# Two mixture-of-experts stages: three more weight units loaded before the router, gathers placed among the expert pairs, and the order of products fixed

## The chip, the cores and the metric

The kernel runs on one core of one Trainium2 chip. The metric is device time in microseconds (us) of one execution, the median of several runs. One execution has also been taken by the hardware profiler; times below that name a place in the run are counted from the first instruction of that execution.

## What is computed

The input is 256 tokens of 1024 numbers (two tiles of 128 tokens), all in float32. Two blocks follow each other. The first has two layers (l = 0, 1), and each layer is

```python
x = layer_norm(ALPHA * x + attention_mixer(x))          # ln1
x = layer_norm(ALPHA * x + moe(x))                      # ln2
```

The mixer joins three kinds of attention and a product with `w_out`. The mixture of experts (moe) sends each token to 2 of 16 experts, chosen by a sigmoid router; an expert is `down(silu(x @ gate) * (x @ up))` with `gate` and `up` of 1024 x 512 and `down` of 512 x 1024. So the weights of an expert are three matrices of 2 MB, 96 MB for the 16 experts of a layer. The second block (two feed-forward layers each with its own mixer and a cross attention to a memory) uses the first block's output, and a matrix `mem_wkv_2`, of which a quarter is multiplied at the beginning and another at the end of each moe stage of the first block.

## The kernel before, in words

The kernel is written in a language in which Python code states the instructions and their data, and a scheduler chooses, for each engine, the order in which they are issued. An instruction stated later can be issued earlier, if its inputs and its buffer are there. `self.after(x)` (L461) fixes an order by hand: the instructions stated inside it come behind x on x's engine. Every engine and every queue works through its own list in order.

**Weights.** Class `Stream` (L82 to L176) holds one list of all weight loads in the order of use. A unit is one DMA of up to 1 MB on SyncE's queue (L122). Units go into one of two rings of 8 KB per partition: `stage` (NSTAGE = 6 slots) and `piece` (NPIECE = 6). For most products a unit in `stage` is split by ScalarE (L146) and VectorE (L147) into a high and a low part, which stand in a slot of `piece`. The units of the experts and of the memory matrix are "raw": they are used as they are, in float32, straight from either ring. An expert unit is half of a matrix, 1 MB; experts of even number use `stage`, those of odd number `piece` (L342, L347). `take` (L165) hands out the next unit, `release` (L172) gives its slot back, and `_load` (L116) issues, in the order of the list, all loads that have a slot. The list of a layer is made in `plan` (L312): the blocks of `w_in`, the other weights of the mixer, four units of `w_out`, two units of the memory matrix, then for each pair of experts four units of `gate`, four of `up` and (one pair later) four of `down`, then the first block of the next weights and two more memory units.

**The mixer's end.** `mixer` (L784) makes its last block of projections at L985, with the low half of its input in buffer `xl`. It turns the queries and keys of the last attention into buffer `m4` (L986 to L992), runs that attention (L994) and multiplies with `w_out` (L1008).

**The router and the gathers.** `moe` (L1173) computes the router, the place of each token in its expert's list of 64 (CAP) tokens, and a selection matrix. `gather(g)` (L1271) multiplies the normalised tokens (buffers `m5` and `m2`) with columns of that matrix and so collects the tokens of four experts into a buffer: `m0`, `m1`, `xh`, `xl` for g = 0 to 3. One gather is 32 products of 256 columns. `memory_gemm` (L1686) is the memory product of this stage's beginning; it is stated at L1292.

**The expert stage.** The loop at L1367 goes over eight pairs of experts and one turn more. A product of a pair runs two experts side by side: expert k writes rows 64k to 64k+63 of the result, so two instructions with 64 weight columns each occupy the two halves of TensorE. In float32 an instruction is shown as two steps. A turn `pr` does: `gate` of pair `pr` (L1316), the transposes of the previous pair's activations (L1332), other work of that turn, the scatter of pair `pr-2` (L1360), `up` of pair `pr` (L1316), `down` of pair `pr-1` (L1345). In turn 0 the other work is gather(1), in turn 1 gather(2), gather(3) and eight pairs of transposes of the selection matrix (L1390) into buffer `m5`. In front of turn 2 a value is loaded and tested (L1369, L1370); the code under the test, `moe_more` (L1424), handles lists of more than 64 tokens and does not run with this input. After the last turn the result is normalised (`LayerNorm.tile` for both tiles, L1404 and L1406), and the memory product of the stage's end is made (L1419).

Of the kernel before, what the change touches and what calls it, by code (L numbers as in the profile page):

```python
# [16 lines left out]
P = 128  # L17
# [6 lines left out]
NSTAGE = 6  # L24
# [57 lines left out]
class Stream:  # L82
# [3 lines left out]
    def __init__(self, nc, stage_pool, piece_pool):  # L86
        self.nc, self.pools = nc, (stage_pool, piece_pool)
# [3 lines left out]
        self.rings = ([], [])  # L91

# [8 lines left out]
    def raw(self, key, ap, a, b, ring):  # L101

        self.units.append(dict(ap=ap, a=a, b=b, left=1, tile=None, ring=ring, first=len(self.pieces)))
        self.pieces.append(dict(key=key, u=len(self.units) - 1, raw=True, n=len(self.pieces)))
# [11 lines left out]
    def _load(self, upto=None):  # L116
        while self.loaded < (upto or len(self.units)):
            u = self.units[self.loaded]
            if not self._room(u["ring"]) or u["ring"] and u["first"] > self.split:
                return  # L120
            u["tile"] = self._tile(u["ring"], u)[:, :u["a"] * u["b"]].rearrange("p (a b) -> p a b", a=u["a"])
# [57 lines left out]
class LayerNorm:  # L179
# [8 lines left out]
    def tile(self, t):  # L188
        k = self.k
        if self.full:  # L190
# [3 lines left out]
            self.copied = k.x_t(self.res[:, t, :], t, self.hi, self.lo, self.g)  # L194
            return
# [56 lines left out]
class Kern:  # L252
    def __init__(self, ctx, tc, I, out, consts_ap, coff, bands_ap, stop=None):
# [23 lines left out]
        self.ws = Stream(nc, self.sp, self.wp)  # L277
# [29 lines left out]

    def sm(self, n, name, dt=F32, bufs=None):
        return self.small.tile([P, n], dt, name=name, tag=name, bufs=bufs)


    def plan(self):  # L312
        I, ws = self.I, self.ws
        for l in range(2):
# [20 lines left out]
            mem(1024 * l)  # L335
            for k in range(9):
                if k < 8:
                    for name in ("gate", "up"):
                        for j0 in (0, 4):
                            for e in (2 * k, 2 * k + 1):  # L340
                                w = I["exp_w_" + name][l, e].rearrange("(p j) n -> p j n", j=8)
                                ws.raw(name, w[:, j0:j0 + 4], 4, 512, e % 2)  # L342
                if k > 0:
                    for c0 in (0, 2):
                        for e in (2 * k - 2, 2 * k - 1):
                            w = I["exp_w_down"][l, e].rearrange("(p c) n -> p c n", c=4)
                            ws.raw("down", w[:, c0:c0 + 2], 2, 1024, e % 2)  # L347
# [152 lines left out]
    def x_t(self, src, t, hi, lo, g=None, b=None):  # L500
# [3 lines left out]
        for q in range(2):  # L504
            p = self.mm()
            for k in range(4):
                nc.tensor.transpose(p[:, k * P:(k + 1) * P], src[:, 4 * q + k:D:8], self.c["ident"])
# [62 lines left out]
    def spread_gb(self, g, b, l):  # L570

        nc = self.nc
        row = self.slot("m1").rearrange("p (k d) -> p k d", k=2)
# [1650 lines left out]
```

## Time and profile before

| | us |
|---|---|
| median of 3 runs | 2030.56 |
| lowest and highest of them | 2025.97, 2030.61 |
| the profiled execution, its own time | 2032.96 |
| its span, first to last instruction | 2031.2 |
| router of layer 0 to its first expert product | 158 to 187.7 |
| expert stage of layer 0, first product to last scatter | 187.7 to 423.0 |
| expert stage of layer 1, first product to last scatter | 602.4 to 837.2 |

TensorE is busy in 96% of the span, VectorE in 56%, ScalarE in 43%; the granted TensorE clock is 0.98 of full speed on the mean. The DMA engines move 453 MB, 223 GB/s on the mean. The share of busy time is a mean over stages with different limits, and an engine counts as busy also where it works at half its width; so the stage that is changed has to be read by itself.

### The profile page before, as it was taken

What the parts mean: (1) busy time and instruction counts of PE and PEld (TensorE: products, weight loads), DVE (VectorE), ACT (ScalarE), POOL (GpSimd) and SP (SyncE); (2) the same over time, 40 slices, a digit from 0 to 9 for tenths busy, and PEclk for the clock granted to TensorE, in tenths of its full rate; (3) what the DMA queues carried; (4) which work ended last, traced back from release to release, by engine and by line L of the source; (5) the groups of instructions that cost most, each with busy time, mean ns of one, the idle gap of its engine ahead of it and who ended that gap; (6) DMA issues with size and microseconds to landing.
All of it is one profiled execution on the core that took longest, in us unless ns stands there. A gap on an engine that the chain in (4) does not pass through costs nothing.

```text
span 2031.2 us, 27990 instructions
## 1 busy us (share of the span) xinstructions
PE 1952.2 (96%) x11069; PEld 1472.9 (73%) x11069; DVE 1128.5 (56%) x2211; ACT 868.5 (43%) x1537; POOL 56.6 (3%) x115
## 2 busy tenths in 40 slices
PE   6999899989999999899999899999999999999999
PEld 6776433358764333389989787899989986778998
DVE  7775122157761122556569776655565567756554
ACT  5553100036632000345456565644454455556442
POOL 1110000000100000000000100000000000000000
PEclk9999999999999999999999999999999997999999
DMA  8347899974469999955555344465555553325551
GB/s 271 138 144 264 351 413 422 420 257 147 146 221 368 393 420 421 361 190 184 194 167 186 105 187 145 146 206 189 185 182 184 187 190 135 125 83 185 188 187 42
DMA packets 175980, 453.39 MB, mean 223 GB/s; under 512 B 11056, under 2 KB 106780, under 8 KB 149084
## 3 DMA queue, kind: packets, MB, share of 16 engines
q1 hardware_dynamic: 172044, 435.55, 58.2%
q0 software_dynamic: 3792, 15.91, 2.2%
q8 instruction: 91, 1.49, 0.3%
q14 instruction: 53, 0.43, 0.1%
HBM read 446.19 MB, written 5.24 MB: 222 GB/s over the span
## 4 chain that ended last, share of the span: by engine, by line
PE 58%; DMA 5%; DVE 3%; ACT 2%; issue 1%; POOL 0%; SPq 0%; DVEq 0%; ACTq 0%; POOLq 0%
PE mm L1563 7%; PE mm L1564 7%; PE mm L1565 7%; PE accb L451 4%; PE accb L450 4%; PE accb L449 4%; PE acca L451 4%; PE acca L450 4%; PE acca L449 4%; PE mm L1316 2%; DMA piece<-in_exp_w_down_dram 2%; DMA piece<-in_exp_w_gate_dram 2%; DMA piece<-in_exp_w_up_dram 1%; DVE piece L147 1%; PE mm L1808 1%; PE acca L1345 1%
## 5 line engine op out<-in xcount | busy, mean ns | idle before, releaser
L147 DVE TENSOR_TENSOR piece<-stage,piece 128x1024 fp32r<-128x1024 f32 (+3 forms) x439 | 514.7, 1181 | 253.6 <-ACT piece L146 251.7
L146 ACT ACTIVATE piece<-stage 128x1024 fp32r<-128x1024 f32 (+3 forms) x439 | 445.6, 1023 | 342.8 <-PE mm L1565 204.1
L1563 PE MATMUL mm<-m,piece 128*128 128x256 f32 x736 | 206.9, 281 | 2.3 <-DVE m L2121 2.3
L1564 PE MATMUL mm<-m,piece 128*128 128x256 f32 x736 | 206.7, 281 | 0.0
L1565 PE MATMUL mm<-m,piece 128*128 128x256 f32 x736 | 206.4, 280 | 0.0
L1563 PE MATMUL mm<-xh,piece 128*128 128x256 f32 x576 | 163.1, 283 | 0.0
L1565 PE MATMUL mm<-xh,piece 128*128 128x256 f32 x576 | 163.0, 283 | 0.0
L1564 PE MATMUL mm<-xl,piece 128*128 128x256 f32 x576 | 163.0, 283 | 0.0
L449 PE MATMUL accb<-piece,m 128*128 128x512 f32 (+1 forms) x364 | 143.8, 396 | 1.2 <-ACT m L916 1.0
L450 PE MATMUL accb<-piece,m 128*128 128x512 f32 (+1 forms) x364 | 144.8, 398 | 0.0
L451 PE MATMUL accb<-piece,m 128*128 128x512 f32 (+1 forms) x364 | 143.7, 395 | 0.5 <-DVE m L459 0.5
L1563 PEld LDWEIGHTS mm<-m,piece 128*128 128x128 f32 x736 | 139.2, 189 | 4.6 <-issue 3.0
L1564 PEld LDWEIGHTS mm<-m,piece 128*128 128x128 f32 x736 | 139.2, 189 | 1.9 <-issue 0.3
L1565 PEld LDWEIGHTS mm<-m,piece 128*128 128x128 f32 x736 | 139.4, 189 | 0.0
L449 PE MATMUL acca<-piece,m 128*128 128x512 f32 (+1 forms) x348 | 137.1, 395 | 1.8 <-ACT m L458 1.6
L450 PE MATMUL acca<-piece,m 128*128 128x512 f32 (+1 forms) x348 | 137.7, 396 | 0.0
L451 PE MATMUL acca<-piece,m 128*128 128x512 f32 (+1 forms) x348 | 137.1, 395 | 0.5 <-DVE m L459 0.5
L1316 PE MATMUL mm<-stage,m 128*64 128x512 f32 x256 | 122.2, 630 | 7.9 <-DVEq L1370 6.3
L1316 PE MATMUL mm<-piece,m 128*64 128x512 f32 x256 | 121.6, 631 | 3.3 <-issue 3.3
L1563 PEld LDWEIGHTS mm<-xh,piece 128*128 128x128 f32 x576 | 110.4, 192 | 1.3
L1564 PEld LDWEIGHTS mm<-xl,piece 128*128 128x128 f32 x576 | 110.4, 192 | 1.2
L1565 PEld LDWEIGHTS mm<-xh,piece 128*128 128x128 f32 x576 | 110.4, 192 | 0.0
(573 smaller groups left out, 3745.0 us busy)
## 6 DMA issues: line engine op xcount, KB each, us to landing
stage<-in_ffn_wi_dram SPq DMA_DIRECT2D x88, 1024.0 KB, 5.4
stage<-in_ffn_wo_dram SPq DMA_DIRECT2D x44, 1024.0 KB, 5.2
stage<-in_exp_w_gate_dram SPq DMA_DIRECT2D x32, 1024.0 KB, 7.0
stage<-in_exp_w_up_dram SPq DMA_DIRECT2D x32, 1024.0 KB, 9.5
piece<-in_exp_w_gate_dram SPq DMA_DIRECT2D x32, 1024.0 KB, 14.6
piece<-in_exp_w_up_dram SPq DMA_DIRECT2D x32, 1024.0 KB, 13.0
stage<-in_exp_w_down_dram SPq DMA_DIRECT2D x32, 1024.0 KB, 15.0
piece<-in_exp_w_down_dram SPq DMA_DIRECT2D x32, 1024.0 KB, 18.8
```

Of the source, the lines that this page charges most:

```text
L146: nc.scalar.activation(wh, src, AF.Copy)
L147: nc.vector.tensor_tensor(wl, src, wh.bitcast(F32), op=OP.subtract)
L449: nc.tensor.matmul(out, ah, bh, start=first, stop=False)
L450: nc.tensor.matmul(out, ah, bl, start=False, stop=False)
L451: return nc.tensor.matmul(out, al, bh, start=False, stop=last)
L1316: mm = nc.tensor.matmul(o[64 * k:64 * k + 64, :], x[:, j, s:s + CAP], w[k][:, jj, :], start=(j == 0), stop=(j == 7))
L1345: nc.tensor.matmul(y[nb][64 * k:64 * k + 64, :], x[:, f, 64 * k:64 * k + 64], w[k][:, cc, nb * 512:(nb + 1) * 512], start=(f == 0), stop=( ...
L1563: nc.tensor.matmul(out, wh[:, j, :], hi[:, j, :], start=(j == 0), stop=False)
L1564: nc.tensor.matmul(out, wh[:, j, :], lo[:, j, :], start=False, stop=False)
L1565: nc.tensor.matmul(out, wl[:, j, :], hi[:, j, :], start=False, stop=(j == 7))
L1808: nc.tensor.matmul(po[:, k * P:(k + 1) * P], v[:, mc, h * 256 + cc * P:h * 256 + (cc + 1) * P], pt[t][:, (2 * h + mc) * P:(2 * h + mc + 1) ...
```

## The change

It has seven parts.

1. NSTAGE is 7 instead of 6, for the whole kernel. The room comes from `dynamic_dma_scratch_size=8192` at the kernel's end.
2. Two units, the first halves of `gate` of experts 0 and 1, no longer use the rings. They go into the buffers `xl` and `m4`, once these are free of the mixer's data (`ws.free += ...` is stated behind L992). In the list the first of them stands in front of the `w_out` units, the second behind them; `_load` stops at such a unit until its buffer has been set free.
3. The other expert units alternate between the rings in a cycle of 13.
4. Inside one `gate`, `up` or `down` every product is put behind the one before it, so the two experts of a pair alternate strictly.
5. gather(2) moves from turn 1 to turn 2 and gather(3) to turn 4. The gathers alternate between `m0` and `m1`. The transposed selection matrix goes to `xl`, the scatter's input to `xh` instead of `m2`, since `m5`, `m2` are needed longer.
6. The test of L1370 moves from turn 2 to turn 4.
7. At the end of the stage the order is fixed: first half of the memory product, transposes of the normalised tile 0, second half of the memory product, transposes of tile 1, then the memory product's copies out. The table for the square root is loaded on ScalarE behind the last `silu`. The memory product's results go to other buffers, and to DRAM in two DMAs of GpSimd's queue instead of one.

```diff
-NSTAGE = 6
+NSTAGE = 7
 class Stream:
+    def raw(self, key, ap, a, b, ring=0, slot=None):
+        self.units.append(dict(ap=ap, a=a, b=b, left=1, tile=None, ring=ring, slot=slot, first=len(self.pieces)))
+        u = len(self.units) - 1
+        if not slot:
+            self.use(key, u)
+        return u
+    def use(self, key, u):
+        self.pieces.append(dict(key=key, u=u, raw=True, n=len(self.pieces)))
     def _load(self, upto=None):
         while self.loaded < (upto or len(self.units)):
             u = self.units[self.loaded]
-            if not self._room(u["ring"]) or u["ring"] and u["first"] > self.split:
+            if u.get("slot"):
+                if u["slot"] not in self.free:
+                    return
+                self.free.remove(u["slot"])
+                t = self.slot(u["slot"])
+            elif not self._room(u["ring"]) or u["ring"] and u["first"] > self.split:
                 return
+            else:
+                t = self._tile(u["ring"], u)
...
     def plan(self):
+            early = lambda e, tag: ws.raw("gate", I["exp_w_gate"][l, e].rearrange("(p j) n -> p j n", j=8)[:, 0:4], 4, 512,
+                                          slot=tag)
+            first = [early(0, "xl")]
             self.plan_rows("w_out", I["w_out"][l].rearrange("(c p) n -> p c n", p=P), 8)
+            first.append(early(1, "m4"))
...
+            def expert(key, ap, a, b):
+                nonlocal n
+                ws.raw(key, ap, a, b, n % (NSTAGE + NPIECE) % 2)
+                n += 1
...
     def mixer(...):
                 nc.vector.tensor_copy(qkfT[:66, k, :, t * P:(t + 1) * P], p[:66].rearrange("p (b n) -> p b n", b=4))
+        ws.free += ["xl", "m4"]
...
     def moe(...):
-            x = self.slot(("m0", "m1", "xh", "xl")[g]).rearrange("p (j n) -> p j n", j=8)
+            x = self.slot(("m0", "m1")[g % 2]).rearrange("p (j n) -> p j n", j=8)
...
         def gate_or_up(kind, pr):
+            prev = []
...
-                        mm = nc.tensor.matmul(o[64 * k:64 * k + 64, :], x[:, j, s:s + CAP], w[k][:, jj, :],
-                                              start=(j == 0), stop=(j == 7))
+                        with self.after(*prev):
+                            mm = nc.tensor.matmul(o[64 * k:64 * k + 64, :], x[:, j, s:s + CAP], w[k][:, jj, :],
+                                                  start=(j == 0), stop=(j == 7))
+                        prev = [mm]
...
         for pr in range(9):
-            if pr == 2:
+            if pr == 4:
                 more = nc.values_load(ovi[0:1, 0:1], min_val=0, max_val=1)
...
             if pr == 1:
-                gather(2)
-                gather(3)
-                ptr = self.slot("m5", F32R).rearrange("p (a n) -> p a n", a=8)
+                ptr.append(self.slot("xl", F32R).rearrange("p (a n) -> p a n", a=8))
...
+            if pr == 2:
+                gather(2)
+            if pr == 4:
+                gather(3)
...
                 scatter(7, y)
-                nxt.tile(0)
-                ready = nxt.copied
-                nxt.tile(1)
...
-        self.memory_gemm(l, 1, "m0", after={0: [state["scatter"]]}, out_after=ready)
+        with self.after(state["silu"]):
+            self.table(AF.Sqrt)
+        def first(at):
+            with self.after(at):
+                nxt.tile(0)
+            return nxt.moved
+        at = self.memory_gemm(l, 1, [m0[:, 512 * t:512 * t + 512] for t in range(2)], {0: [state["scatter"]]}, first, l)
+        with self.after(at):
+            nxt.tile(1)
+        self.memory_out(nxt.copied)
...
-    nc = _bacc.Bacc("TRN2", target_bir_lowering=False, num_devices=1)
+    nc = _bacc.Bacc("TRN2", target_bir_lowering=False, num_devices=1, dynamic_dma_scratch_size=8192)
```

`down` gets the same chain of `self.after(*prev)`; `moe_more` is rewritten for the new buffers.

## Rows read from the trace of the kernel before

**Rows 1.** The page: the span in 40 slices of 50.8 us, DMA's busy tenths.
```profile
DMA  8347899974469999955555344465555553325551
```

**Rows 2.** Stretches of layer 0's expert stage: busy time by engine, clock, DMA share, GB/s.
```profile
190.00:200.00 10.00, 10.00 (x53) 5.01 (x50) 0.78 (x3) 1.73 (x3) 0.00 (x0) 0.89 0.54 203
200.00:220.00 20.00, 20.00 (x114) 10.23 (x113) 4.50 (x9) 3.51 (x7) 0.00 (x0) 1.00 0.97 395
220.00:240.00 20.00, 20.00 (x112) 9.88 (x110) 3.59 (x7) 5.07 (x10) 0.00 (x0) 1.00 0.76 303
240.00:260.00 20.00, 13.68 (x54) 5.35 (x53) 4.46 (x7) 1.55 (x3) 0.00 (x0) 0.83 0.95 382
...
340.00:360.00 20.00, 19.65 (x82) 7.96 (x80) 5.49 (x8) 1.20 (x2) 0.00 (x0) 1.00 1.01 420
```

**Rows 3.** DMA issues of 187 to 424 us: count, KB each, median us to landing.
```profile
piece<-in_exp_w_down_dram SPq DMA_DIRECT2D x16, 1024.0 KB, 18.8
stage<-in_exp_w_up_dram SPq DMA_DIRECT2D x14, 1024.0 KB, 12.2
...
stage<-in_exp_w_gate_dram SPq DMA_DIRECT2D x12, 1024.0 KB, 14.0
```

**Rows 4.** SyncE's queue in order of time: start us, us, what.
```profile
60.90 34.53 SPq L122 DMA_DIRECT2D stage<-in_w_out_dram  x4
...
193.61 0.33 SPq L122 DMA_DIRECT2D stage<-in_exp_w_up_dram  x1
...
197.04 0.33 SPq L122 DMA_DIRECT2D stage<-in_exp_w_up_dram  x1
...
396.11 0.33 SPq L122 DMA_DIRECT2D piece<-in_exp_w_down_dram  x1
```

**Rows 5.** TensorE in order of time, start of layer 0's expert stage.
```profile
187.66 1.11 PE L1316 MATMUL mm<-stage,m 128*64 128x512 f32 x1
187.67 1.11 PE L1316 MATMUL mm<-piece,m 128*64 128x512 f32 x1
...
195.99 0.59 PE L1316 MATMUL mm<-stage,m 128*64 128x512 f32 x1
...
196.42 0.59 PE L1316 MATMUL mm<-stage,m 128*64 128x512 f32 x1
...
196.94 0.39 PE L1282 MATMUL mm<-gv,m 128*128 128x256 f32 x1
...
201.12 0.64 PE L1316 MATMUL mm<-stage,m 128*64 128x512 f32 x1
...
246.90 1.08 PE L1316 MATMUL mm<-stage,m 128*64 128x512 f32 x1 [6.32 <-DVEq L1370]
```

**Rows 6.** TensorE's groups of 187 to 424 us: busy us, mean ns, idle before.
```profile
L1360 PE MATMUL mm<-m,m 128*128 128x512 f32 x64 | 22.3, 442 | 1.9 <-DVE res L1362 0.6
...
L1332 PE MATMUL tp<-ident,prob 128*128 128x128 f32 x32 | 6.0, 310 | 0.1
```

**Rows 7.** TensorE in order of time, end of layer 0's expert stage.
```profile
420.28 2.81 PE L1360 MATMUL mm<-m,m 128*128 128x512 f32 x8
...
434.60 1.97 PE L507 MATMUL mm<-ident,res 128*128 128x128 f32 x8 [5.31 <-DVE res L562]
```

**Rows 8.** Stretches of layer 1's expert stage, columns as in rows 2.
```profile
640.00:660.00 20.00, 15.87 (x69) 5.03 (x69) 2.13 (x3) 1.97 (x4) 0.00 (x0) 1.00 0.78 311
660.00:680.00 20.00, 19.19 (x73) 8.14 (x74) 3.08 (x5) 0.60 (x1) 0.00 (x0) 0.83 0.93 349
```

**Rows 9.** Stretches ahead of layer 0's expert stage, columns as in rows 2.
```profile
125.00:146.00 21.00, 19.50 (x115) 15.02 (x114) 17.54 (x59) 12.50 (x36) 0.00 (x0) 1.00 0.38 144
...
173.00:193.00 20.00, 20.00 (x103) 13.25 (x103) 11.97 (x32) 4.93 (x7) 2.84 (x5) 0.83 0.41 119
```

**Rows 10.** TensorE in order of time: `w_out` products, and the last attention's end.
```profile
123.57 0.40 PE L449 MATMUL accb<-piece,m 128*128 128x512 f32 x1
...
144.58 0.50 PE L1134 MATMUL tp<-pt,m 128*64 128x128 f32 x3
```

More of the change, by code (lines that the diff above doesn't have):

```diff
@@ L91, in __init__ @@
         self.rings = ([], [])
+        self.free = []
     def unit(self, ap, a, b):
@@ L340, in plan @@
                             for e in (2 * k, 2 * k + 1):
+                                if first:
+                                    ws.use("gate", first.pop(0))
+                                    continue
                                 w = I["exp_w_" + name][l, e].rearrange("(p j) n -> p j n", j=8)
-                                ws.raw(name, w[:, j0:j0 + 4], 4, 512, e % 2)
+                                expert(name, w[:, j0:j0 + 4], 4, 512)
                 if k > 0:
@@ L346, in plan @@
                             w = I["exp_w_down"][l, e].rearrange("(p c) n -> p c n", c=4)
-                            ws.raw("down", w[:, c0:c0 + 2], 2, 1024, e % 2)
+                            expert("down", w[:, c0:c0 + 2], 2, 1024)
             if l == 0:
@@ L568, in ln_gain, with spread_gb @@
         self.nc.vector.tensor_tensor(v, v, gb[1], op=OP.add)
[L570 removed]
+    def spread_gb(self, g, b, l, tag):
         nc = self.nc
[L573 removed]
+        row = self.slot(tag).rearrange("p (k d) -> p k d", k=2)
         for k, v in enumerate((g, b)):
@@ L1291, in moe @@
             ln.gain(rows)
-        self.memory_gemm(l, 0, "xl", {7: [at_pp]})
+        self.memory_gemm(l, 0, [self.prob()[:, 0:512] for t in range(2)], {7: [at_pp]})
         p = self.tp()
@@ L1683, in memory_load, with memory_gemm @@
         self.nc.gpsimd.dma_start(self.mem_t, self.memT)
-    def memory_gemm(self, k, b, tag, after={}, out_after=()):
-        o = self.slot(tag)[:, 0:D].rearrange("p (t d) -> p t d", t=2)
-        acc = [self.acc(), self.acc()]
+    def memory_gemm(self, k, b, out, after={}, mid=None, pair=None):
+        acc = [self.acc(pair), self.acc(pair)]
         x = self.mem_t.rearrange("p (j n) -> p j n", j=8)
@@ L1691, in memory_gemm @@
             for j in range(8):
+                if j == 4 and mid:
+                    order.enter_context(self.after(mid(at)))
                 if j in after:
@@ L1696, in memory_gemm, with memory_out @@
                 for t in range(2):
-                    self.nc.tensor.matmul(acc[t], x[:, j, t * P:(t + 1) * P], w[:, j % 4, :], start=(j == 0), stop=(j == 7))
+                    at = self.nc.tensor.matmul(acc[t], x[:, j, t * P:(t + 1) * P], w[:, j % 4, :], start=(j == 0), stop=(j == 7))
                 if j % 4 == 3:
                     self.ws.release()
-        with ExitStack() as order:
-            order.enter_context(self.after(*out_after))
+        self.mem_out = (k, b, acc, out)
+        if not mid:
+            self.memory_out()
+        return at
+    def memory_out(self, after=()):
+        k, b, acc, out = self.mem_out
+        with self.after(*after):
             for t in range(2):
-                self.nc.scalar.activation(o[:, t, :], acc[t], AF.Copy, scale=self.mem_r[:, t:t + 1])
-        self.nc.gpsimd.dma_start(self.memKV[k].rearrange("p (t d) -> p t d", t=2)[:, :, b * 512:(b + 1) * 512], o)
+                self.nc.scalar.activation(out[t], acc[t], AF.Copy, scale=self.mem_r[:, t:t + 1])
+        for t in range(2):
+            self.nc.gpsimd.dma_start(self.memKV[k][:, 1024 * t + 512 * b:1024 * t + 512 * b + 512], out[t])
     def memory_keys(self):
```

72 lines of the change are left out of this document (42 added, 30 removed).

## Prediction, written before the changed kernel was run

> **What bounds the kernel now.** I read first the 40 slices of the page, because the mean of 223 GB/s hides that transfers bound one kind of stage only. In slices 5 to 7 and 12 to 16 the DMA engines are busy nine tenths or more, elsewhere mostly three to six [rows 1]. These are the two expert stages, where 96 MB of weights pass through a layer. I read them next in stretches. From 190 to 260 us the transfers are not yet steady: 203, 395, 303 and 382 GB/s; by 340 they run at 420 with a share of 1.01, and that is the ceiling [rows 2]. A unit of 1024 KB [rows 3] then takes 1.049 MB / 421 GB/s = 2.49 us.
>
> Third, the queue and TensorE. The first expert product starts at 187.66 [rows 5]; all 12 ring slots are full by then, and SyncE issues the next load only at 193.61, when the first half of `gate` has released its two units [rows 4]. Of the 96 units of a layer, 84 are issued in the stage (2 x (16 + 14 + 12) [rows 3]). The last goes out at 396.11 [rows 4] and, at the group's median of 18.8 us [rows 3], lands at about 414.9. The last scatter starts at 420.28 and ends at 423.1 [rows 7]. So **the end of the stage is set by the DMA stream**: its restart, its holes, and its number of units. Where it has holes is seen in the same stretches. Against 421 GB/s, the stretch to 200 us, counted from 193.61, lacks 1.6 us, the next three lack 1.2, 5.6 and 1.8 us, 10.2 together [rows 2]. Check: 193.61 + 84 x 2.49 + 10.2 = 413.0, against 414.9; 1.9 us remain unexplained, and I keep them. The large hole falls where two gathers and the transposes of the selection matrix follow each other and no product releases a slot; the stretch from 240 holds the test of L1370, where TensorE stands 6.32 us [rows 5]. Layer 1 repeats this, with 311 and 349 GB/s in the two stretches behind its gathers [rows 8].
>
> **The change part by part, for one layer.**
>
> *Three more units ahead of the router.* 81 instead of 84 units remain for the stage: -3 x 2.49 = -7.5 us. They have to be loaded earlier, and there is room: from 125 to 146 us the DMA share is 0.38, from 173 to 193 it is 0.41 [rows 9]; three units need 7.5 us of about 25 idle ones. `xl` and `m4` come free by 145 at the latest, where the mixer's last attention ends [rows 10]. Cost nothing; if that cover were gone, the gain of 7.5 would be.
>
> *The restart comes later.* The two early units hold `xl` and `m4`, which are no ring slots, so the first half of `gate` now releases nothing that a load waits for. The next release is that of the second half, for which SyncE issues at 197.04 in the trace of before [rows 4]: +3.4 us.
>
> *Gathers and test moved.* Releases now follow each other every eight steps of 0.43 us (195.99 to 196.42 [rows 5]), 3.4 us for two units that take 5.0 us to load. The stream stays fed, except across gather(1), 196.94 to 201.12 [rows 5]: the two units issued at 197 last 5.0 us, the next release comes at 204.5, a hole of about 2.5. With the 1.6 of the start, 4.1 instead of 10.2: -6.1. Gather(2), gather(3) and the test then stand where 13 slots have been refilled. Up to eight loads are out at a time (18.8 / 2.49 is 7.5 [rows 3]), enough to cover the test's 6.3 us.
>
> *Sum of the stream:* 197.04 + 81 x 2.49 + 4.1 + 1.9 = 404.8, which is 10.1 earlier than 414.9.
>
> *Behind the last landing* comes the last half of `down`, eight steps or 3.4 us, and the scatter, 2.8 [rows 7]: 411.0. Before, the trace has 8.2 us from that landing to the end; I put the other 2 us down to products of single experts in the way, which the fixed order excludes.
>
> *TensorE's own floor.* With the order fixed every product runs paired (187.66 and 187.67 start together [rows 5]). A pair of experts is 3 x 16 steps of 0.43, 20.6 us; eight are 165. Scatters 22.3, transposes 6.0 [rows 6], three gathers of 4.2, 16 transposes of the selection matrix 3.0 (half of the 32), the test 6.3, and twice the slow steps: 187.66 to 196.42 is 8.8 for 15 steps, 2.3 more than at 0.43 [rows 5]; the granted clock is 0.83 in the test's stretch [rows 2]. Together 220, which ends at 407.6. That is only 3 us below the stream's end, so waits of the two add up in places. I take **412, 11 us earlier**. The bounds: a gain of 15.5, if TensorE's floor were the end, and of 4, if each pair costs TensorE 1 us more than summed (waits of scatters for VectorE among them), 415.6 plus the 3.4 by which stream and floor could add.
>
> *The end of the stage.* Second half of the memory product (16 steps, 6.9 us) behind the transposes of tile 0 instead of mostly there already; TensorE still stands idle until VectorE has normalised tile 0 (5.31 us [rows 7]). The same products and the same wait: 0, bounds -1.5 and +1.5. What VectorE does first of the two tiles can shift by one 1.3 us step.
>
> *Queues and the rest.* Two early loads and one more `stage` unit are issued on SyncE in places where it only waits for slots. GpSimd issues one DMA more per memory product; nothing behind it is due for tens of us. The table load of the square root was in ScalarE's idle time and stays there. The seventh slot elsewhere: DMA is at three to six tenths there [rows 1], so nothing. The smaller scratch of GpSimd's DMAs: the trace shows no cost; 0 to +1. The kernel's start loads one unit more ahead of other constants: 0 to +2.
>
> **Sum.** Two layers of -11: -22. The profiled execution of 2032.96 would become 2011; it lies 2.4 above the median of 2030.56, so the median would become **2009**.
>
> **A rule that speaks against it.** With strict order TensorE stops at every missing unit: in the steady part a half needs 3.4 us of TensorE and 5.0 us of the stream, a wait of up to 1.6. Before, single products filled that time: TensorE is busy 19.65 of 20 us from 340 on, at a granted clock of 1.00, while after the longer stand of the test the clock is 0.83 on the mean of that stretch [rows 2]. The Trainium skill, page "TensorE: Matmul & The Clock Gate", section "Loop structure matters more than you think", warns of exactly this loop, a DMA wait ahead of each product, after which the matmuls run cold. As a mechanism of this kernel: if each wait of the last three pairs (nine, one per `gate`, `up`, `down`) brought the 2.3 us of slow steps [rows 5], 21 us, less the 14 us of slack that these waits are, would be lost: 7 of a layer's 11, time about 2023. No row shows a fall of the clock after so short a wait.
>
> **Rivals.**
> A. *TensorE becomes the bound.* Its floor is close, the order of other work is the scheduler's, and a gather or scatter in a bad place delays releases. For it: the hole that one bad place made before (5.6 us [rows 2]). Against it: floor and stream agree within 3 us only where nothing is lost. A gain of 5 per layer: 2020; the clock's rule gives nearly the same (2023) and stands here as a case of its own below.
> B. *Slow clock by short waits*, above: 2023.
> C. *It does not do what it says*: the early units come so late, or the stream stalls at a new place (13 slots used in strict turn), that holes and restart eat the gain: 2030.
> D. *Slower.* `_load` stops at the early unit in front of `w_out` until the mixer has stated that `xl` is free. Before, SyncE issues the `w_out` loads from 60.90 on [rows 4]. Should they be issued only behind the last attention, at about 145 [rows 10], then 4 + 2 + 15 units, 52 us, would follow, up to 197, 9 us behind the stage's present start; and the `w_out` products, which now begin at 123.57 [rows 10], would begin 21 us late. Between the two I take 16; per layer +16 - 11, in all 2041. It decides at one point: whether the first `w_out` load stands before about 120 us. Against it: the scheduler issues by readiness, and the buffers it needs are free at 60.
>
> **Numbers.** Chances: forecast 0.62, A 0.18, B 0.04, C 0.09, D 0.07. About 0.3% (6 us) can be told from no change. A and B (2020, 2023) are faster than 2024.5, so faster is 0.62 + 0.18 + 0.04 = 0.84, less 0.02 for an A or B that comes out worse: 0.82; the same 0.09 + 0.02 = 0.11; slower 0.07. The range reaches from 1998 (11 more, 4.5 per layer to TensorE's floor and 1 of the end) to 2027 (A and B and their spread); D, most of C and the tails, 2 in 10, lie outside. The forecast's own range is 1999 to 2018.
>
> **What would show it.** Right: the first issue of the stage near 197, one stretch of 20 us at most below 380 GB/s, the last `down` issued some 10 us earlier, the last scatter ending near 412 and 11 earlier in layer 1; the first `w_out` load still near 60. Wrong: TensorE busy without waits for DMA to the end and a stream with holes (A); PEclk under 1 after 340 (B); a stage start later than 187.7, or `w_out` products that begin after 125 (D).

## The result, and the profile after

The changed kernel takes 2001.76 us (median of 4 runs, 1998.24 to 2002.3), the kernel before 2029.57 beside it: a ratio of 0.9862, 95% interval 0.9845 to 0.988, or 27.8 us less. The forecast was 22 less, 2009 in a range of 1998 to 2027, with 0.82 on faster. The profiled execution has a span of 2000.5 us, before 2031.2: 30.7 less.

The page, the two lines on the DMA engines (busy tenths and GB/s in 40 slices):

```profile
DMA  8456999973569999855564353455555543335550
GB/s 290 145 203 229 397 419 420 421 256 123 206 236 403 420 421 421 300 187 181 186 202 137 132 219 109 163 190 190 190 200 186 182 165 137 127 99 175 190 190 22
```

In each expert stage four slices now run at 397 to 421 GB/s; in [rows 1] the first stage begins with an 8 and the second needs a fifth 9. The same in stretches of layer 0's stage, columns as in [rows 2], then one stretch of layer 1 that answers to [rows 8]:

```profile
190.00:200.00 10.00, 10.00 (x63) 5.80 (x61) 2.33 (x5) 3.92 (x6) 0.00 (x0) 1.00 0.54 205
200.00:210.00 10.00, 10.00 (x49) 3.26 (x47) 0.82 (x2) 0.00 (x0) 0.00 (x0) 1.00 0.78 301
210.00:220.00 10.00, 10.00 (x57) 4.60 (x55) 0.69 (x1) 2.66 (x5) 0.00 (x0) 1.00 1.01 422
220.00:240.00 20.00, 20.00 (x111) 9.53 (x107) 4.46 (x7) 3.76 (x7) 0.00 (x0) 1.00 1.02 423
...
640.00:660.00 20.00, 20.00 (x88) 6.95 (x87) 4.27 (x7) 1.19 (x2) 0.00 (x0) 1.00 1.02 422
```

From 210 us on nothing is lost. What is left of the holes stands before: 1.6 us between the restart and 200, and 10 x (1 - 301/421) = 2.9 across gather(1). The granted clock is 1.00 in every one of these stretches.

SyncE's queue, which answers to [rows 4]:

```profile
56.81 8.04 SPq L137 DMA_DIRECT2D stage<-in_w_out_dram  x4
...
122.49 0.33 SPq L137 DMA_DIRECT2D xl<-in_exp_w_gate_dram  x1
...
135.80 0.33 SPq L137 DMA_DIRECT2D m<-in_exp_w_gate_dram  x1
...
193.50 0.33 SPq L137 DMA_DIRECT2D stage<-in_exp_w_up_dram  x1
...
383.54 0.33 SPq L137 DMA_DIRECT2D stage<-in_exp_w_down_dram  x1
```

All four `w_out` loads go out by 65 us; the two early units go out as `xl` and `m4` come free; the stage's first issue is at 193.50 and its last at 383.54, 12.6 us sooner than before.

TensorE in order of time, start and end of layer 0's stage (answers to [rows 5, 7]):

```profile
185.02 1.11 PE L1352 MATMUL mm<-xl,m 128*64 128x512 f32 x1
...
193.41 0.39 PE L1317 MATMUL mm<-gv,m 128*128 128x256 f32 x1
...
406.48 1.02 PE L1386 MATMUL acca<-stage,m 128*64 128x512 f32 x2
...
409.28 0.97 PE L1401 MATMUL mm<-xh,xl 128*128 128x512 f32 x3 [0.72 <-ACT xh L488]
410.52 0.49 PE L1401 MATMUL mm<-xh,xl 128*128 128x512 f32 x1 [0.28 <-DVE xh L489]
412.85 1.03 PE L1401 MATMUL mm<-xh,xl 128*128 128x512 f32 x2 [1.83 <-DVE res L1403]
413.67 8.45 PE L1758 MATMUL acca<-stage,m 128*128 128x512 f32 x16
421.95 1.04 PE L541 MATMUL mm<-ident,res 128*128 128x128 f32 x8
422.83 7.03 PE L1758 MATMUL acca<-piece,m 128*128 128x512 f32 x16
...
430.51 0.42 PE L483 MATMUL accb<-piece,xh 128*128 128x384 f32 x1
```

The last scatter (L1401) is now drawn out over 6.4 us and is no good mark for the end of the stage. I count from the first `gate` product to the end of the last `down` product (L1386) as the stage, and from there to the first product of the next weights (L483) as its end:

| us | before | after | less |
|---|---|---|---|
| up to the first gate product, layer 0 | 187.7 | 185.0 | 2.7 |
| stage, layer 0 | 232.6 | 222.5 | 10.1 |
| its end | 25.6 | 23.0 | 2.6 |
| mixer and router of layer 1 | 156.4 | 155.1 | 1.3 |
| stage, layer 1 | 232.2 | 222.3 | 9.9 |
| its end | 26.8 | 25.3 | 1.5 |
| second block | 1169.9 | 1167.3 | 2.6 |

The stages gave 20 of the 30.7 us, close to the 22 of the forecast. The other 10 come from places that the forecast put at nothing. The second block is left aside: in the runs below it takes from 1162.7 to 1170.2 us. The twelve profiles with seven slots have 1165.1 on the mean, the two with six 1169.9 and 1170.2, so the slot may have a share in it; no run separates that.

### The profile page after: what moved, and what is told of

The parts are those of the page before. It is cut to its first block, busy times and chain, and to the rows that moved or that the text cites. A ratio compares the mean times of both kernels' runs of the same rounds, so it can differ in the third digit from the quotient of the medians.

```text
span 2000.5 us, 28009 instructions
## 1 busy us (share of the span) xinstructions
PE 1935.0 (97%) x11069; PEld 1458.6 (73%) x11069; DVE 1127.0 (56%) x2211; ACT 866.9 (43%) x1539; POOL 58.0 (3%) x119
## 4 chain that ended last, share of the span: by engine, by line
PE 56%; DMA 5%; DVE 3%; ACT 2%; issue 0%; POOL 0%; DVEq 0%; SPq 0%; POOLq 0%; ACTq 0%
PE mm L1623 7%; PE mm L1625 7%; PE mm L1624 7%; PE accb L485 5%; PE accb L484 5%; PE accb L483 4%; PE acca L485 4%; PE acca L484 4%; PE acca L483 4%; DMA piece<-in_exp_w_gate_dram 2%; DMA piece<-in_exp_w_down_dram 1%; DMA stage<-in_exp_w_down_dram 1%; DMA stage<-in_exp_w_up_dram 1%; DVE piece L162 1%; PE mm L1876 1%; PE mm L541 1%
## 5 line engine op out<-in xcount | busy, mean ns | idle before, releaser
L162 DVE TENSOR_TENSOR piece<-stage,piece 128x1024 fp32r<-128x1024 f32 (+3 forms) x439 | 513.8, 1179 | 240.9 <-ACT piece L161 239.3
L1352 PE MATMUL mm<-stage,m 128*64 128x512 f32 x512 | 221.8, 595 | 0.0
L1352 PE MATMUL mm<-piece,m 128*64 128x512 f32 x480 | 215.1, 596 | 2.0 <-DMA piece<-in_exp_w_up_dram 2.0
L483 PE MATMUL accb<-piece,m 128*128 128x512 f32 (+1 forms) x364 | 143.1, 394 | 0.9 <-ACT m L950 0.7
L483 PE MATMUL acca<-piece,m 128*128 128x512 f32 (+1 forms) x348 | 138.2, 398 | 0.2
L1352 PEld LDWEIGHTS mm<-stage,m 128*64 128x64 f32 x512 | 65.1, 137 | 76.4 <-issue 73.8
L1623 PEld LDWEIGHTS mm<-xh,piece 128*128 128x128 f32 x576 | 110.4, 192 | 1.3
## 6 DMA issues: line engine op xcount, KB each, us to landing
stage<-in_exp_w_up_dram SPq DMA_DIRECT2D x34, 1024.0 KB, 11.2
```

What stands on the lines that cost most here:

```text
L162: nc.vector.tensor_tensor(wl, src, wh.bitcast(F32), op=OP.subtract)
L483: nc.tensor.matmul(out, ah, bh, start=first, stop=False)
L1352: mm = nc.tensor.matmul(o[64 * k:64 * k + 64, :], x[:, j, s:s + CAP], w[k][:, jj, :], start=(j == 0), stop=(j == 7))
L1623: nc.tensor.matmul(out, wh[:, j, :], hi[:, j, :], start=(j == 0), stop=False)
```

## Experiments

All twelve runs in one table: the start of layer 0's stage, stages and ends as defined above in the profiled execution, the median, and the ratio to the kernel before with its interval. An interval is about 4 us to either side, so the stages and ends tell more than the times. Of these, layer 0's stage repeats within 0.1 us where nothing in it was edited (after, after_again, old_end, late_splits); the start of the stage differs by up to 3.2 us and layer 1's stage by up to 2.3 between executions of the same instructions.

| run | start | stages | ends | median | ratio |
|---|---|---|---|---|---|
| (before) | 187.7 | 232.6, 232.2 | 25.6, 26.8 | 2029.57 | |
| (after) | 185.0 | 222.5, 222.3 | 23.0, 25.3 | 2001.76 | 0.9862 (0.9845 to 0.988) |
| after_again | 186.6 | 222.5, 224.6 | 23.1, 25.7 | 2003.17 | 0.9868 (0.9846 to 0.9891) |
| no_early | 186.5 | 223.3, 223.9 | 23.8, 25.7 | 2007.76 | 0.9888 (0.9865 to 0.9911) |
| early_up | 185.3 | 219.8, 220.7 | 23.0, 25.7 | 1999.85 | 0.9855 (0.9832 to 0.9879) |
| feed | 186.2 | 217.7, 219.6 | 24.2, 26.8 | 1995.81 | 0.9833 (0.9811 to 0.9855) |
| gathers_only | 187.3 | 225.8, 227.4 | 25.6, 25.9 | 2016.96 | 0.9943 (0.9926 to 0.9961) |
| seven_only | 184.6 | 230.0, 230.9 | 26.3, 26.2 | 2022.43 | 0.9977 (0.9964 to 0.9989) |
| old_end | 183.4 | 222.5, 222.3 | 24.0, 25.2 | 1999.59 | 0.9869 (0.9846 to 0.9891) |
| no_pin | 186.7 | 222.8, 225.4 | 25.7, 25.8 | 2005.43 | 0.9888 (0.9868 to 0.9908) |
| late_splits | 184.9 | 222.5, 224.2 | 19.6, 19.6 | 1994.58 | 0.9831 (0.9807 to 0.9855) |
| feed_late | 185.2 | 217.8, 218.4 | 19.5, 19.6 | 1981.73 | 0.9778 (0.9755 to 0.98) |
| light | 184.8 | 222.5, 225.0 | 23.0, 25.8 | 2003.36 | 0.988 (0.9861 to 0.9899) |
| no_pin_late | 184.9 | 222.7, 223.3 | 19.6, 19.6 | 1992.18 | 0.9836 (0.9813 to 0.9859) |

Layer 1's 2.3 us go with TensorE's clock at the start of the stage. Its first 4 us in after and in after_again (granted clock in the third column from the right):

```profile
585.62:589.62 4.00, 4.00 (x21) 1.43 (x22) 0.33 (x2) 0.00 (x0) 0.00 (x0) 1.00 0.69 258
```

```profile
588.19:592.19 4.00, 4.00 (x11) 1.24 (x12) 0.33 (x2) 0.00 (x0) 0.00 (x0) 0.50 0.48 186
```

The first half of the first `gate`, eight steps, takes 3.5 us in after and old_end (stage 222.3 in both), 5.7 in late_splits (224.2) and 5.9 in after_again (224.6). So below I compare stages whose first eight steps took about as long.

**What an early unit is worth.** First the changed kernel again:

> The changed kernel once more, as the measure for the other runs of this group. Both theories: 2002 us within 3, 0.986 of the kernel before.

2003.17, as expected. Then without the early units:

```diff
-            first = [early(0, "xl")]
+            first = []
-            first.append(early(1, "m4"))
```

> The changed kernel without the two early units: all 13 slots hold units of the ring, 83 instead of 81 are left for the stage. Theory (the stream's end is restart + units x 2.49 us + holes): +5.0 us per layer for two units; but the first half of gate now frees two slots, so the stream restarts when that half ends, 3.5 us sooner (189.9 instead of 193.4 in the changed kernel's trace), and with four units out before gather(1) instead of two the hole across it shrinks from 2.9 to 1.4. Sum 0.0 per layer: 2002, within 3 of the changed kernel. So the two units would have been worth nothing where they are. Rival (the number of units alone counts, as the forecast's term of -7.5 for three units has it): +10, 2012.

Stages 223.3 and 223.9, against 222.5, 222.3, 222.5 and 224.6 in the two profiles of the changed kernel: 0.6 us longer on the mean, where counting units asks for 5.0. Even this is about what the clock at the start makes: the first eight steps take 6.0 us in layer 0 (4.9 and 5.2 in the changed kernel), and 5.2 in layer 1 (3.5 and 5.9). The restart and the hole stand in SyncE's queue and in the stretches of this run:

```profile
192.69 0.33 SPq L137 DMA_DIRECT2D stage<-in_exp_w_up_dram  x1
```

```profile
200.00:210.00 10.00, 10.00 (x49) 3.45 (x49) 1.91 (x4) 0.56 (x1) 0.00 (x0) 1.00 0.93 366
```

The first issue is 6.2 us behind the stage's start instead of 8.5, and from 200 to 210 the stream moves at 366 GB/s instead of 301. So the two units pay for what they save, within a few tenths. The median is 4.6 us above that of the changed kernel beside it, but the intervals overlap; of the 8.2 us between the two profiled executions 7.3 lie in the second block (1170.2 against 1162.9), where nothing was edited.

If the cost of an early unit is that it frees no slot, then it should be used later, where loads are waiting in the queue anyhow:

```diff
-            early = lambda e, tag: ws.raw("gate", I["exp_w_gate"][l, e].rearrange("(p j) n -> p j n", j=8)[:, 0:4], 4, 512,
+            early = lambda e, tag: ws.raw("up", I["exp_w_up"][l, e].rearrange("(p j) n -> p j n", j=8)[:, 4:8], 4, 512,
                                           slot=tag)
...
-                                if first:
-                                    ws.use("gate", first.pop(0))
+                                if first and name == "up" and j0 == 4:
+                                    ws.use("up", first.pop(0))
```

> The two early units are the second halves of up of experts 0 and 1 instead of the first halves of gate; same buffers, same number of units. Theory: the stream restarts at 190.0 instead of 193.5, the holes are 1.4 across gather(1) and 1.8 where the second half of up frees nothing, 3.2 together instead of 2.9: -3.2 us per layer, 1995. Rival (TensorE is the bound of the stage, when its weights come does not matter): 2002, within 2.

Stages 219.8 and 220.7. With equally long first steps (5.2 us in layer 0 as in after_again, 3.5 in layer 1 as in after) that is 2.7 and 1.6 us shorter, where 3.2 was expected. The median, 1999.85, lies between the theory's 1995 and the rival's 2002 and nearer to the rival; for the theory speak the stages alone. The next run takes away the hole as well:

```diff
-            if pr == 0:
+            if pr == 1:
                 gather(1)
-            if pr == 1:
+            if pr == 2:
                 ptr.append(self.slot("xl", F32R).rearrange("p (a n) -> p a n", a=8))
...
-            if pr == 2:
+            if pr == 3:
                 gather(2)
```

> As the run before (early units are second halves of up), and gather(1) in turn 1, the transposes of the selection matrix in turn 2, gather(2) in turn 3. Theory: restart 190.0; five releases of two units come before gather(1), 25 us of stream, which reach to 214.9, and the next release is at 215.6: hole 0.7 instead of 2.9. -3.5 -2.2 = -5.7 us per layer, 1990. Rival (TensorE's own floor, which the forecast put at 3 us below the stream's end, holds from here on): no more than 3 us below the run with early units in up.

```profile
190.00:200.00 10.00, 10.00 (x50) 3.36 (x48) 0.00 (x0) 1.88 (x2) 0.00 (x0) 1.00 0.75 291
200.00:210.00 10.00, 10.00 (x44) 3.02 (x40) 1.07 (x3) 0.00 (x0) 0.00 (x0) 1.00 1.01 420
210.00:220.00 10.00, 10.00 (x63) 6.29 (x64) 2.87 (x5) 2.85 (x5) 0.00 (x0) 1.00 0.91 353
```

The stretch from 200 has no hole; the one behind it, where gather(1) now stands, loses 1.6 us and not 0.7. Stages 217.7 and 219.6: with equally long first steps (5.2, 6.1) 4.8 and 5.0 shorter than in after_again, instead of 5.7. The rival, no more than 3 us between this run and early_up, is not excluded by the times (4.0 between the medians). TensorE's waits for weights in layer 0's stage (us in total, times, longest) are all in one row:

```profile
PE accb L1386 <- DMA piece<-in_exp_w_down_dram: 0.4, 1, 0.4
```

In the changed kernel they are 2.5 us, below. So in layer 0 a faster stream could shorten this run's stage by hardly more than 0.4: here TensorE's own work begins to bound it, as the rival says. Whether it did so already in the changed kernel, another run has to say: light, below.

**The parts by themselves.** Gathers and test alone: the changed kernel with six slots, no early units, no fixed orders.

```diff
-NSTAGE = 7
+NSTAGE = 6
...
-            first = [early(0, "xl")]
+            first = []
...
-            first.append(early(1, "m4"))
...
-                        with self.after(*prev):
+                        with self.after(*([])):
...
+                nxt.tile(0)
+                ready = nxt.copied
+                nxt.tile(1)
```

> Of the change only parts 5 and 6, with their buffers: six stage slots, no early units, no fixed order of products, the old order at the end. Theory (holes of the stream): 84 units as before; of the holes of before (1.6, 1.2, 5.6, 1.8 us) the last two go, -7.4 us per layer: the stage from first gate product to last down product becomes 225.1 instead of 232.5, the time about 2015. Rival (the number of units ahead of the router carries the gain, as it has the largest term in the forecast, and the placing of gathers only moves waits): stage 230 or more, time 2025 or more.

```profile
200.00:220.00 20.00, 20.00 (x105) 8.49 (x106) 2.79 (x6) 3.79 (x7) 0.00 (x0) 1.00 0.97 395
220.00:240.00 20.00, 20.00 (x100) 7.57 (x97) 2.83 (x4) 1.80 (x3) 0.00 (x0) 1.00 1.01 422
240.00:260.00 20.00, 19.76 (x99) 8.96 (x97) 6.07 (x11) 3.46 (x6) 0.00 (x0) 1.00 1.01 420
```

The holes of 5.6 and 1.8 us are gone, the one across gather(1) is the same 395 GB/s as in [rows 2]. Stages 225.8 and 227.4, 6.8 and 4.8 shorter than before where 7.4 was expected, time 12 us below before: the theory holds in the main, and this is the largest part of the change. What the gathers and what the test give of it was not separated. The stage starts at 187.3, as before, and the queue says why:

```profile
60.54 34.57 SPq L137 DMA_DIRECT2D stage<-in_w_out_dram  x4
```

The seventh slot alone, in the kernel before:

```diff
-NSTAGE = 6
+NSTAGE = 7
...
-    nc = _bacc.Bacc("TRN2", target_bir_lowering=False, num_devices=1)
+    nc = _bacc.Bacc("TRN2", target_bir_lowering=False, num_devices=1, dynamic_dma_scratch_size=8192)
```

> The kernel before with a seventh stage slot and the smaller scratch, nothing else. Theory: one unit less in the stage, -2.5 us per layer, stage 230.0 instead of 232.5; and the stage starts some 2 us sooner, because the fourth w_out load no longer waits (in the changed kernel it is issued at 64.5 instead of 95.4): -7, 2023. Rival (the hole of 5.6 us empties the ring anyway, so that a unit more makes the hole shorter or nothing at all, and the start owes nothing to the slot): stage 232, time 2029.

```profile
57.36 8.04 SPq L122 DMA_DIRECT2D stage<-in_w_out_dram  x4
```

```profile
220.00:240.00 20.00, 16.97 (x82) 6.26 (x80) 2.34 (x4) 3.83 (x7) 0.00 (x0) 0.98 0.75 301
```

Stages 230.0 and 230.9, one unit less, with the hole (301 GB/s) where it was. The stage starts at 184.6, and `w_out` is issued in 8 us instead of 34.5. Seven slots start at 183.4 to 186.7 in all twelve profiles, 185.3 on the mean, six at 187.3 and 187.7: the earlier start is the slot's, by some 2 us.

The order at the end undone (the table load behind the last `silu` goes with it):

```diff
                 scatter(7, y)
+                nxt.tile(0)
+                ready = nxt.copied
+                nxt.tile(1)
...
-        at = self.memory_gemm(l, 1, [m0[:, 512 * t:512 * t + 512] for t in range(2)], {0: [state["scatter"]]}, first, l)
-        with self.after(at):
-            nxt.tile(1)
-        self.memory_out(nxt.copied)
+        at = self.memory_gemm(l, 1, [m0[:, 512 * t:512 * t + 512] for t in range(2)], {0: [state["scatter"]]}, hold=True)
+        self.memory_out(ready)
```

> The changed kernel with the order of before at the end of the stage: both tiles are normalised and transposed without a place fixed by hand, the memory product is stated behind. Theory (read from the traces, from the last down product to the first product of the next block: 25.6 and 26.8 us before, 23.0 and 25.3 after): +2.6 and +1.5, 2006. Rival (the forecast: the order at the end is worth 0 within 1.5; the shorter end comes from splits of the next block that stand elsewhere on VectorE): 2002, ends of 23 and 25.5 us as in the changed kernel.

My theory fell. The time is 1999.59, the ends are 24.0 and 25.2 us. Layer 0's end is 1.0 longer than that of the changed kernel, but with the order at the end as changed it is 23.8 and 24.2 in no_early and feed too; layer 1's is no longer. So the order at the end is worth nothing that can be told from this spread, as the forecast had it, and the shorter end of layer 0 must come from another part.

The fixed order of products undone, `with self.after(*prev)` left out in `gate_or_up` and in `down`:

> The changed kernel without the fixed order inside gate, up and down. Theory: the scheduler's own order is nearly the same here, products run paired but for some downs; stage 222.5 within 1, time 2002 within 2. Rival (the forecast's 2 us per layer for products of single experts in the way of the last half of down): stage 224.5, time 2006.

The median, 2005.43, is nearer to the rival's. But layer 0's stage is 222.8, so paired products are nothing that the fixed order gave here. It is the end of layer 0 that is longer, 25.7, as in the kernel before. VectorE in order of time, first of this run, then of the changed kernel (L1403 residual add, L162 splits of the next block's weights, L592 start of the normalisation):

```profile
410.75 0.68 DVE L1403 SCALAR_TENSOR_TENSOR res<-res,mm 128x512 f32<-128x512 f32 x1
411.34 1.82 DVE L162 TENSOR_TENSOR piece<-stage,piece 128x768 fp32r<-128x768 f32 x2
413.08 0.68 DVE L1403 SCALAR_TENSOR_TENSOR res<-res,mm 128x512 f32<-128x512 f32 x1
413.67 1.82 DVE L162 TENSOR_TENSOR piece<-stage,piece 128x768 fp32r<-128x768 f32 x2
415.41 1.28 DVE L1403 SCALAR_TENSOR_TENSOR res<-res,mm 128x512 f32<-128x512 f32 x2
```

```profile
408.04 1.83 DVE L162 TENSOR_TENSOR piece<-stage,piece 128x768 fp32r<-128x768 f32 x2
...
410.38 1.81 DVE L162 TENSOR_TENSOR piece<-stage,piece 128x768 fp32r<-128x768 f32 x2
412.12 2.48 DVE L1403 SCALAR_TENSOR_TENSOR res<-res,mm 128x512 f32<-128x512 f32 x4
414.52 1.87 DVE L592 BATCH_NORM_STATS2 bnst<-res 128x6 f32<-128x512 f32 x3
```

Without the fixed order, and before, two splits stand between the first and second residual add and two between the second and the rest; with it all four come sooner. In both the normalisation waits for them, and it starts no sooner with the fixed order: 7.1 us behind the last `down` product in this run (416.60 - 409.47), 7.0 in the changed kernel (414.52 - 407.50). TensorE's rows of this run show where the 2.7 us lie:

```profile
412.09 7.11 PE L1758 MATMUL acca<-stage,m 128*128 128x512 f32 x16
423.71 1.97 PE L541 MATMUL mm<-ident,res 128*128 128x128 f32 x8 [4.52 <-DVE sq_y L530]
425.48 9.09 PE L1758 MATMUL acca<-piece,m 128*128 128x512 f32 x16
```

The transposes of tile 0 (L541) start 14.2 us behind the last `down` product here and 14.5 in the changed kernel. But here TensorE has stood still for 4.52 us before them, and its granted clock is 0.50 from 423.71 to 428: eight transposes take 1.97 us instead of 1.04, the second half of the memory product 9.09 instead of 7.03. In the changed kernel the waits are short and lie in the scatter; the slow steps fall into the first half of the memory product (8.45 instead of 7.11), while VectorE is still normalising, and what comes behind runs at full speed. So the fixed order did not shorten VectorE's chain; it moved TensorE's slow steps into a time that was waited for anyhow, which was not planned.

**The end of the stage.** In both kernels the splits stand ahead of the normalisation. If the end waits for them, they should leave the chain:

```diff
-                if pr == 8:
-                    with self.after(state["silu"], state["tr"]):
-                        ws.go(4)
...
         with self.after(at):
             nxt.tile(1)
+        with self.after(self.ln_end):
+            ws.go(4)
```

with `self.ln_end` the last instruction of `ln_full`, and the two memory units of the stage's end ahead of the next weights in `plan`.

> The changed kernel; the four splits of the next block's first weights, which VectorE makes between or ahead of the last residual adds, are put behind the normalisation of tile 1, and the two memory units stand ahead of those weights in the list of loads. Theory (from the last down product to the next block, VectorE's chain of residual adds and normalisation is what ends last; the splits stand in it with 3.6 us in layer 0 and 4.7 in layer 1): the ends shrink from 23.0 and 25.3 us to 20.3 and 21, 7 us in all, 1995. Rival (TensorE's own 32 memory products set the end, or the next block then waits for its splits): 2002, within 2, with a wait of the first product of the next block for a split.

```profile
407.35 2.80 PE L1401 MATMUL mm<-xh,xl 128*128 128x512 f32 x8
410.00 7.03 PE L1757 MATMUL acca<-stage,m 128*128 128x512 f32 x16
418.35 1.16 PE L541 MATMUL mm<-ident,res 128*128 128x128 f32 x8 [1.33 <-DVE sq_y L530]
419.35 7.03 PE L1757 MATMUL acca<-piece,m 128*128 128x512 f32 x16
```

The last scatter is in one piece again, the transposes of tile 0 (L541) start 10.9 us behind the last `down` product instead of 14.5, and both ends are 19.6 us; 1994.58. The ends are 3.4 and 5.7 us shorter, more than the 7 of the theory together. In layer 0 all of it is VectorE's earlier end. In layer 1 the transposes start 4.4 us sooner behind the last `down` product; the rest is that TensorE now waits 1.33 us instead of 4.04 before them and no slow steps follow (the second half of the memory product takes 7.03 us instead of 7.62, the first transposes 1.16 instead of 1.97). The same with the fixed order of products taken out:

> The run with the late splits, without the fixed order inside gate, up and down. Theory (the fixed order won its 3 us only because the scheduler then put the next block's splits ahead of the last residual adds in layer 0): with the splits behind the normalisation anyway, the ends are 19.6 us in both layers and the stages 222.5 to 225, the time 1995 within 2. Rival (the fixed order itself is worth 3 us, by products of single experts in the way): 1998 or more, with stages or ends longer than in the run with late splits.

Ends of 19.6, stages of 222.7 and 223.3, 1992.18: with the splits out of the way, the fixed order is worth nothing. And both improvements together:

> The run feed (early units as second halves of up, gather(1) in turn 1, transposes in turn 2, gather(2) in turn 3) with the late splits. Theory: the two gains add, 1995.8 - 7 = 1989. Rival (the stream's gain at the end of the stage is taken back because the memory units, loaded earlier, and the next weights share the stream): 1994 or more.

Stages 217.8 and 218.4, ends 19.5 and 19.6, **1981.73 us**, ratio 0.9778 to before (0.9755 to 0.98): 20 us below the changed kernel and the best of all. It lies 7 below the sum because feed's ends were longer than those of the changed kernel that the theory took: from 24.2 and 26.8 they shrink by 11.9 us, not by 7. With layer 1's stage, 1.2 shorter, this gives 1982.8.

**Whether TensorE or the stream bounds the stage.** The scatters of four pairs are left out:

```diff
-            if pr > 1:
+            if pr in (2, 7, 8):
                 scatter(pr - 2, y)
```

> The changed kernel with the scatters of pairs 1 to 4 left out (so the outputs of those experts are not added): TensorE has 4 x 2.8 = 11.2 us less to do in each stage, in turns 3 to 6, where the stream already runs at 420 GB/s. Theory (the stream bounds the stage): stage 222.4 less at most 1.5, time within 3 of the changed kernel, and the time saved turns up as waits of TensorE for weights. Rival (TensorE bounds it, as its waits of only 6.6 us in 222.5 suggest): stage 211 to 214, time 1982 or less.

Layer 0's stage is 222.5, to the tenth as long as with the scatters; layer 1's is 225.0, not shorter either (222.3 and 224.6 with them). TensorE's waits in layer 0's, of this run and then of the changed kernel (us in total, times, longest; those for DMA, and in the second the test's, L1411):

```profile
PE mm L1352 <- DMA piece<-in_exp_w_up_dram: 2.9, 3, 1.3
PE acca L1386 <- DMA stage<-in_exp_w_down_dram: 2.6, 2, 1.3
PE mm L1352 <- DMA stage<-in_exp_w_up_dram: 2.5, 2, 1.3
PE accb L1386 <- DMA piece<-in_exp_w_down_dram: 2.4, 2, 1.3
```

```profile
PE accb L1386 <- PEq L1411: 1.5, 1, 1.5
PE mm L1352 <- DMA piece<-in_exp_w_up_dram: 1.3, 1, 1.3
...
PE accb L1386 <- DMA piece<-in_exp_w_down_dram: 1.0, 1, 1.0
```

With two more rows of 1.3 there and one of 0.2 here, the waits for DMA are 13.0 us against 2.5: of the 11.2 that TensorE was spared, 10.5 came back as waits for weights. The stream bounds the changed kernel's stage, and an engine that waits only 6.6 of 222.5 us, 2.5 of them for weights, was still not the bound.

## Why the prediction was right, and where it was not

**The restart** was forecast 3.4 us later for a fixed start. Behind the first `gate` product it is at 8.5 us (193.50 - 185.02) instead of 5.95 (193.61 - 187.66): +2.5, the term's mechanism, smaller by 0.9 because the first `gate` took 8.4 us (185.02 to 193.41) instead of 9.3 (187.66 to 196.94 [rows 5]); its slow steps ended sooner.

**Three units, -7.5.** Each unit counted is right: seven_only gives 2.6 and 1.3 us for one. But for the two early ones the term does not stand alone: no_early shows that restart and gather hole take back all but 0.6 at most of their 5.0 us. The forecast had those two prices in its sum, so its total holds; it did not see that they belong to these units, and so that the units sat in the wrong place.

**Holes, 4.1 instead of 10.2.** Measured 1.6 + 2.9 = 4.5. gathers_only shows the two large ones gone by the placing alone, which makes it the change's main part.

**The stream's end, 404.8.** The last `down` product was to end 3.4 us later, at 408.2, which is 220.5 behind the forecast's start of 187.66; it ends at 407.5, which is 222.5 behind the real start: right within 2 us (that the two times, counted from the first instruction, agree better, within 0.7, is the earlier start's doing). The last scatter, named as the sign at 412, ends at 413.9, because splits had moved in front of it.

**TensorE's floor, 220, "only 3 us below".** The distance held, but its sum did so by luck. Without the waits for weights the stage would be 222.5 - 2.5 = 220.0 us up to the last `down` product, 2.5 less than the stream makes it. The sum carried over the test's 6.3 us, where at its new place the test costs TensorE 1.5. Against that it had too little work: less the test and the last scatter it comes to 220 - 6.3 - 2.8 = 211, where TensorE has 222.5 - 6.6 = 216. light shows that with 11 us less of it the stage is as long, so rival A did not happen here; in feed, whose stages are 5 us shorter, it begins to.

**The slow clock, rival B.** In the steady part the clock is 1.00 with waits of up to 1.3 us, and in light it stays 1.00 with 13 us of them: no fall. But at one place it does show, the drawn-out scatter at the end:

```profile
414.00:418.00 4.00, 4.00 (x7) 1.59 (x7) 4.00 (x7) 0.30 (x1) 0.00 (x0) 0.69 1.06 379
```

After waits of 0.72, 0.28 and 1.83 us the granted clock falls, to 0.69 on the mean of 4 us, so for more than half of them it is at 1.2 of 2.4 GHz, and the 16 memory products that follow take 8.45 us; in late_splits, with the scatter in one piece, 7.03. Of these 1.4 us the end sees some 0.4: VectorE's last step for tile 0 ends only at 421.56, and the transposes start at 421.95. Behind the one wait of 4.52 us in no_pin the slow clock costs the end 3 us. The section "Loop structure matters more than you think" of the page "TensorE: Matmul & The Clock Gate" in the Trainium skill speaks of a long DMA wait ahead of every matmul. No run here shows that case: the waits for DMA in the expert loop are short and no fall follows them, and the falls at the end stand behind waits for ScalarE and VectorE.

**The seventh slot elsewhere: "nothing".** Wrong by 2.7 us between these two profiles, by some 2 on the mean of all: DMA at three to six tenths does not mean that no load waits for a slot. The fourth `w_out` load waited from 60.90 to 95 [rows 4]. Rival D, later `w_out` loads, went the other way for the same reason. That the earlier load is what moves the start was not isolated from the rest of what the slot does; that the slot moves it, was.

**The end, 0 within 1.5.** The order at the end is worth 0 within these bounds, as argued (old_end). But the ends shrank by 2.6 and 1.5. "The same products and the same wait" left out that products behind a wait of 5.31 us [rows 7] run slower: there eight transposes took 1.97 us, in the changed kernel 1.04. In layer 0 it was the fixed order of products that broke this wait up. The forecast credited it with 2 us behind the last landing; it gives none there (no_pin, no_pin_late), so the 2.6 are luck. Layer 1's 1.5 can't be put down to a part: without late splits its end takes 25.2 to 26.8 us in all runs. The forecast had looked at how TensorE waited for VectorE and not at what VectorE did meanwhile: 3.6 us of splits inside the chain. Without them, in late_splits, the ends are 3.4 and 5.7 us shorter.

So of the 30.7 us between the profiles the forecast's 22 were 20 in the stages, for the reasons that it named, except the early units, which pay for what they save. The rest came from two terms set at nothing, and in part, in the second block, from a place that no run explains.

## What to carry to other kernels

A load made early into a buffer of its own saves its transfer only if it is used where the queue is backed up: at the head of a stage it frees no slot, and the stream restarts later by what it saved. Place the work that frees nothing (gathers, tests) where the ring has just been refilled. Where one engine waits for another at a stage's end, read what the other does in that time: optional work that the scheduler may put inside the chain should be put behind it by hand. And compare what runs behind such a wait: here a wait of 4.5 us cost TensorE 3 us more behind it.

## What was not expected of the hardware

The test costs TensorE 6.32 us in front of turn 2 in layer 0 [rows 5] and 3.35 in layer 1, and 1.2 to 2.5 in front of turn 4 in all the runs that have it there, for code that is not run; why, stays open. Identical instructions start the stage from 183.4 to 186.7 us with seven slots, and the number of slow steps behind the start differs between executions: none in layer 1 of after, five to six in after_again, whose stage there is 2.3 us longer.
